# Tile 3's selection made in the front stage, and tile 3 fourth in the attention's order

## The chip, the core and the metric

The kernel runs on one core of a Trainium2 chip. Time is device time in microseconds (us). The kernel before takes 2221.42 us, the median of three runs (2221.03 to 2222.13). One more execution was taken with the hardware profiler; all rows come from it. The engines are TensorE (PE in the rows, PEld for its weight loads), VectorE (DVE), ScalarE (ACT), GpSimd (POOL), and SyncE (SP), which here only issues transfers.

## What is computed

One layer over 2048 tokens of width 1024: a projection, three mixers whose outputs are joined (a causal convolution, a sparse attention and a pooling mixer), an output projection, and a mixture of experts. The change touches the attention. Each query scores all allowed keys with eight small indexer heads, keeps the 256 best, and attends to those alone:

```python
def block(args):
    qa, qib, wib, bi = args
    qchunk = (bi * Q_BLOCK + jnp.arange(Q_BLOCK)) // CHUNK
    allowed = key_chunk[None, :] <= qchunk[:, None]
    rel = jax.nn.relu(jnp.einsum('bqhd,bsd->bqhs', qib, ki).astype(jnp.float32))
    score = jnp.einsum('bqhs,bqh->bqs', rel, wib.astype(jnp.float32)) * idx_scale
    score = jnp.where(allowed[None], score, -jnp.inf)
    _, idx = lax.top_k(score, topk)
    kv_sel = jax.vmap(lambda a, i: a[i])(ckv, idx)
    logits = jnp.einsum('bqhc,bqkc->bqhk', qa, kv_sel).astype(jnp.float32) * att_scale
    valid = (idx // CHUNK) <= qchunk[None, :, None]
    logits = jnp.where(valid[:, :, None, :], logits, -jnp.inf)
    p = jax.nn.softmax(logits, axis=-1).astype(kv_sel.dtype)
    return jnp.einsum('bqhk,bqkc->bqhc', p, kv_sel)
```

The kernel does not gather keys: it finds for each query the score of the 256th best key, and adds a mask (0, or a large negative number) to the logits of all keys.

## The kernel before

The program runs through a front stage (to about 460 us), the attention (460 to 1132), the output projection, and the experts (to 2215). The front goes three times over the tokens: convolution and pooling inputs, then latents, keys and values, and last, in `sweep3`, the indexer's queries. `sweep3` takes four chunks c of 512 tokens; for each it multiplies the reloaded activations h with weights (three matmuls for one product, lines 92 to 94: high x high, low x high, high x low parts), 96 matmuls a chunk, 384 in all, into small PSUM banks called sm. ScalarE takes the high part of each result (qsh), VectorE the low part (qsl), and both are written to DRAM (qi_d of the chunk, line 597). The front's convolution (line 630, an add of one tap over 512 tokens, on VectorE) and its transposes and normalisation run beside.

The attention has 16 query tiles of 128 queries; tile t sees (t + 1) x 128 keys. Per tile there are four parts, written as generators that yield after each step:

- `scores` loads the queries (qi, line 857), and for each of eight heads and each block of 512 keys does two matmuls (lines 862, 863), a relu on ScalarE (rel, line 865) and a weighted sum on VectorE (into S, line 866).
- `threshold` finds the 256th best: mean and deviation (line 892), five tries, each a count of the entries over a guess (tries 0 and 2 a Sign on ScalarE, the others line 922 on VectorE) and a chain of small operations on GpSimd that makes the next guess; then an exact pick (ScalarE line 957, VectorE line 958 and MAX8, line 961) and the mask (line 966).
- `logits`, for two heads at a time (a group g): loads of qa (line 1015) and kc (line 1022), matmuls (line 1028), mask and row maximum on VectorE (line 1029), Exp on ScalarE (line 1034).
- `context`: transposes of the probabilities (line 1067), copies to SBUF (pT, line 1069), products with the values vc (loaded in line 1063, multiplied in line 1054), and at the end of a tile the scaling and the write.

`attention` weaves them by a list of positions: at position p it runs the context of tile `ORDER[p]`, the logits one group ahead, the scores of `ORDER[p + 3]`, and the thresholds of `ORDER[p + 1]` and `ORDER[p + 2]`. From the second position on it also weaves in `modrows`, two steps a group: 32 loads of 512 KB of the modulation weights mod_w (line 180) and their matmuls (line 201). Tiles 0 and 1 need no selection, as they see at most 256 keys. Tile 2's is made ahead: the generator `ahead` runs its `scores` and `threshold` in `sweep3`, five steps behind each product of the chunks c > 1, in small buffers of one copy each (their names begin with e: eS, erel, ecj, ebias) and in the banks sm. All other tiles have theirs in the attention.

Tiles, pools and generators fix which instructions exist and on which buffers; a scheduler then puts each engine's instructions in one fixed order, and each engine runs its list in that order, with waits for what others produce. SyncE's transfers are such a list too: one that waits holds those behind it.

## Time and profile before

| | |
|---|---|
| median of three runs | 2221.42 us |
| profiled execution: time / span | 2217.02 / 2215.0 us |
| mean granted TensorE clock | 0.964 of full |
| busy: TensorE / VectorE / ScalarE / GpSimd | 2001.5 / 1569.5 / 1220.0 / 889.0 us |
| bytes moved, mean rate | 569.65 MB, 257 GB/s |

The profile's rows give for an instruction its line, the engine, the tiles it writes and reads (out<-in), its shape and time; in brackets the idle time of the engine just before it and what ended that. A window's row gives the busy time of each engine in that stretch, the granted TensorE clock as a share of full speed, the mean busy share of the 16 DMA engines and the rate. Tile rows run from the copy that ends one tile's context (line 1079) to the next tile's: the row of tile t then holds its context and, woven in, the next tile's logits. All positions are in us from the span's start.

### The profile page before, as it was taken

To read this page: it belongs to the slowest core of one execution; us is meant where nothing else is said; L and a number is where in the kernel's file an instruction comes from. 1 tells how busy PE (TensorE), PEld (TensorE's weight loads), DVE (VectorE), ACT (ScalarE), POOL (GpSimd) and SP (SyncE) were. 2 spreads that over 40 slices of the span, in tenths; PEclk is the share of its full clock that TensorE was granted. 3 is DMA by queue.
4 is the path that set the end of the run, shared out by engine and by line. 5 is a ranking of instruction groups with operands and counts; after the bars stand their busy time and mean duration, and the time that the engine had idled before them with its cause. 6 is when DMAs were issued, how large, how long until landed. Compare 5 with 4: busy or idle time off the path is not lost. (4 is left out here: it accounts for less than half of the span.)

```text
span 2215.0 us, 37651 instructions
## 1 busy us (share of the span) xinstructions
PE 2001.5 (90%) x12857; PEld 1509.4 (68%) x12858; DVE 1569.5 (71%) x3004; ACT 1220.0 (55%) x2039; POOL 889.0 (40%) x1599
## 2 busy tenths in 40 slices
PE   5899999988899999988889997799999999999984
PEld 4677887865667777766768775567777666666762
DVE  5696888768888888996436555666767666766673
ACT  4733333256777788877642222556666565665552
POOL 4442112446544433474000113435555455555443
PEclk9999999989999999999999998799999999999987
DMA  8636979859986666768867435799999899999894
GB/s 288 242 132 205 285 217 291 304 173 295 290 252 213 206 209 194 231 212 271 230 211 268 153 125 198 268 320 361 353 298 337 265 345 321 335 326 314 302 301 145
DMA packets 314388, 569.65 MB, mean 257 GB/s; under 512 B 36467, under 2 KB 149576, under 8 KB 313160
## 3 DMA queue, kind: packets, MB, share of 16 engines
q1 hardware_dynamic: 289560, 489.79, 66.0%
q0 software_dynamic: 22304, 68.41, 10.8%
q10 hardware_dynamic: 2320, 8.91, 1.0%
q8 instruction: 105, 1.72, 0.3%
q14 instruction: 99, 0.81, 0.1%
HBM read 462.44 MB, written 103.53 MB: 256 GB/s over the span
## 5 line engine op out<-in xcount | busy, mean ns | idle before, releaser
L1732 DVE TENSOR_TENSOR wl<-wr,wh 128x1024 fp32r<-128x1024 f32 x314 | 386.5, 1267 | 157.6 <-ACT wh L1731 151.6
L1731 ACT ACTIVATE wh<-wr 128x1024 fp32r<-128x1024 f32 x372 | 373.4, 1053 | 207.4 <-PE acc L94 162.4
L93 PE MATMUL acc<-wl,xh 128*128 128x512 f32 (+3 forms) x544 | 219.9, 405 | 4.2 <-DVE wl L1732 4.1
L1029 DVE CUSTOM_DVE_ANT_0 L<-pl,bias 128x512 f32<-128x512 f32 (+3 forms) x312 | 180.2, 607 | 60.5 <-PE pt L1067 34.0
L92 PE MATMUL acc<-wh,xh 128*128 128x512 f32 (+3 forms) x544 | 217.3, 409 | 5.4 <-ACT wh L1731 5.1
L94 PE MATMUL acc<-wh,xl 128*128 128x512 f32 (+3 forms) x544 | 216.6, 401 | 0.0
L1028 PE MATMUL pl<-kc,qa 128*128 128x512 f32 (+3 forms) x640 | 180.4, 386 | 20.2 <-DMA kc<-kh_d 9.4
L1069 ACT ACTIVATE pT<-pt 128x512 f32<-128x512 f32 (+1 forms) x288 | 158.0, 575 | 64.8 <-PE pt L1067 64.0
L1732 POOL TENSOR_TENSOR wl<-wr,wh 128x1024 fp32r<-128x1024 f32 x58 | 145.3, 2562 | 106.1 <-ACT wh L1731 104.2
L866 DVE SCALAR_TENSOR_TENSOR S<-rel,wi,S 128x512 f32<-128x512 f32 (+3 forms) x259 | 171.3, 681 | 22.5 <-ACT rel L865 21.8
L1067 PE MATMUL pt<-identr,L 128*128 128x128 f32 x1088 | 170.1, 282 | 17.2 <-ACT pT L1069 12.9
L865 ACT ACTIVATE rel<-pi 128x512 f32<-128x512 f32 (+3 forms) x296 | 153.9, 549 | 46.5 <-PE pi L863 28.8
L630 DVE SCALAR_TENSOR_TENSOR ac<-u,kc,ac 128x512 f32<-128x512 f32 x240 | 176.9, 778 | 0.1
L1067 PEld LDWEIGHTS pt<-identr,L 128*128 128x128 f32 x1088 | 126.3, 143 | 55.8 <-ACT pT L1069 22.2
L1034 ACT ACTIVATE L<-L,ast 128x128 f32<-128x128 f32 (+15 forms) x128 | 154.1, 1204 | 13.3 <-DVE ast L1033 13.0
L1054 PE MATMUL po<-pT,vc 128*64 128x128 f32 x2176 | 145.9, 281 | 12.4 <-ACT pT L1069 12.2
L1054 PEld LDWEIGHTS po<-pT,vc 128*64 128x64 f32 x2176 | 120.5, 139 | 42.0 <-ACT pT L1069 27.4
L862 PE MATMUL pi<-kk,qi 128*128 128x512 f32 (+3 forms) x296 | 127.7, 433 | 19.3 <-ACT rel L865 16.7
L1028 PEld LDWEIGHTS pl<-kc,qa 128*128 128x128 f32 x640 | 108.7, 193 | 50.2 <-DVE ast L1029 16.8
L92 PEld LDWEIGHTS acc<-wh,xh 128*128 128x128 f32 (+3 forms) x544 | 98.8, 183 | 41.9 <-ACT wh L1731 10.9
L93 PEld LDWEIGHTS acc<-wl,xh 128*128 128x128 f32 (+3 forms) x544 | 100.0, 184 | 38.6 <-issue 6.9
L1782 POOL DMA_INDIRECT x_d<-yo,ent x31 | 90.0, 2905 | 82.4 <-DVE yo L1825 57.8
(562 smaller groups left out, 4641.9 us busy)
## 6 DMA issues: line engine op xcount, KB each, us to landing
wr<-in_exp_w_dram SPq DMA_DIRECT2D x256, 512.0 KB
wr<-in_exp_w_dram SPq DMA_DIRECT2D x64, 1024.0 KB
h<-h_d SPq DMA_DIRECT2D x64, 512.0 KB
vc<-v_d SPq DMA_DIRECT2D x112, 256.0 KB
h_d<-h POOLq DMA_DIRECT2D x32, 512.0 KB
qa<-qa_d SPq DMA_DIRECT2D x128, 128.0 KB
modr<-in_mod_w_dram SPq DMA_DIRECT2D x32, 512.0 KB
xt<-in_x_dram SPq DMA_DIRECT2D x16, 512.0 KB
```

Source lines behind the costliest of these rows:

```text
L92: mm(out, lh, rh, start=start, stop=False)
L93: mm(out, lh, rl, start=False, stop=False)
L94: mm(out, ll, rh, start=False, stop=stop)
L630: nc.vector.scalar_tensor_tensor(acc[j], src, kc[:, j, i:i + 1], acc[j], op0=OP.mult, op1=OP.add)
L866: nc.vector.scalar_tensor_tensor(S[:, s:e], r[:, :e - s], self.wi[:, t, h:h + 1], S[:, s:e] if h else self.tie[:, s:e], op0=OP.mult, op1=O ...
L1028: nc.tensor.matmul(ps[:, :e - s], q[:, h % 2, m], k[:, s:e], start=m == 0, stop=m == 1)
L1029: nc.vector.tensor_tensor_reduce(L[:, s:e], ps[:, :e - s], bias[:, s:e], 1.0, -3e38, OP.add, OP.max, mx[:, i:i + 1])
L1054: nc.tensor.matmul(po[r], v[:, (k2 + i) % 4, r], pT[:, i, j], start=len(left) > 2 * t, stop=len(left) <= 2)
L1067: nc.tensor.transpose(pt[:, i, j], P[j][:, (k2 + i) * 128:(k2 + i + 1) * 128], self.ident)
L1069: nc.scalar.activation(pT[:, :m], pt[:, :m], AF.Copy)
L1731: nc.scalar.activation(H[:, s], W[:, s], AF.Copy)
L1732: (nc.gpsimd if pool else nc.vector).tensor_tensor(L[:, s], W[:, s], H[:, s].bitcast(F32), OP.subtract)
```

## The change

`ahead` makes two selections one behind the other, tile 2's and then tile 3's, advanced three steps behind each product of the chunks c = 1, 2 and 3 in place of five for c = 2 and 3. In `ORDER` tile 3 goes from the last place to the fourth. The writes of qi_d of chunk 1 go from GpSimd's queue to SyncE's. The small buffers are 512 wide in place of 384; ebias gets two copies, one for each tile; the bf16 output of the counts (cj) shares erel with the relus and the pick. `scores` in `attention` now skips tiles 0 to 3. At the position of tile 2 no scores are woven in any more; tile 8's, which stood there, stand at tile 3's.

```diff
@@ -594,9 +594,9 @@
                     for m in range(2):
                         a, b = slice(m * 64, m * 64 + 64), slice(64 - m * 64, 128 - m * 64)
                         for to, q in (a, hi), (b, lo):
-                            (nc.sync if c > 1 else nc.gpsimd).dma_start(self.qi_d[c][to, 2 * (j + i) + m, :], q[a].bitcast(F32))
-                    if c > 1:
-                        self.advance(early, 5)
+                            (nc.sync if c else nc.gpsimd).dma_start(self.qi_d[c][to, 2 * (j + i) + m, :], q[a].bitcast(F32))
+                    if c:
+                        self.advance(early, 3)
                     self.spend(side, 5)
         for _ in early:
             pass
@@ -722,7 +722,7 @@
             if "y" in self.dbg:
                 nc.sync.dma_start(self.dbg["y"][c, 2 + j], y)
 
-    ORDER = (0, 1, 2, 6, 7, 8, 9, 10, 11, 12, 13, 14, 15, 5, 4, 3)
+    ORDER = (0, 1, 2, 3, 6, 7, 8, 9, 10, 11, 12, 13, 14, 15, 5, 4)
     TRIES = 5
     SIGN = (0, 2)
 
@@ -731,20 +731,23 @@
     def work(self, pool, width, dtype, tag, bufs):
 
         if self.small:
-            tag = "e" + ("rel" if tag == "R" else tag)
-            return self.aq.tile([128, min(width, self.small)], dtype, name=tag, tag=tag,
-                                bufs=1)
+            tag = "e" + ("rel" if tag in ("R", "cj") else tag)
+            return self.aq.tile([128, min(width, 512)], dtype, name=tag, tag=tag, bufs=2 if tag == "ebias" else 1)
         return getattr(self, pool).tile([128, width], dtype, name=tag, tag=tag, bufs=bufs)
 
+    AHEAD = (2, 3)
+
     def ahead(self):
 
-        self.small, self.masks = 384, {}
-        S = self.work("ats", T, F32, "S", 1)
-        for part in self.scores(2, S), self.threshold(2, S):
-            for _ in part:
-                self.small = None
-                yield
-                self.small = 384
+        self.masks = {}
+        for t in self.AHEAD:
+            self.small = True
+            S = self.work("ats", T, F32, "S", 1)
+            for part in self.scores(t, S), self.threshold(t, S):
+                for _ in part:
+                    self.small = None
+                    yield
+                    self.small = True
         self.small = None
 
     def bank(self, tag, bufs, shape=(128, 512)):
@@ -784,7 +787,7 @@
 
             def scores(i):
 
-                if i < NT and order[i] >= 3:
+                if i < NT and order[i] > self.AHEAD[-1]:
                     t = order[i]
                     S = self.ats.tile([128, T], F32, name="S", tag="S", bufs=3)
                     thr[i] = self.threshold(t, S)
```

After the change the lines from 731 on are numbered three higher.

The scheduler's order on TensorE, at tile 2's scores in the front stage. Before (kk are the keys, qi the queries, h the activations of the products), the end of tile 2's eight heads, which stand behind 240 of the 384 products:

```order
1438 L862 MATMUL sm<-kk_1773,qi 128x384
1439 L863 MATMUL sm<-kk_1774,qi 128x384
1440 L862 MATMUL sm<-kk_1773,qi 128x384
1441 L863 MATMUL sm<-kk_1774,qi 128x384
1442 L650 MATMUL cm<-identr,ac_3179 128x128
1443 L650 MATMUL cm<-identr,ac_3180 128x128
1444 L862 MATMUL sm<-kk_1773,qi 128x384
1445 L863 MATMUL sm<-kk_1774,qi 128x384
1446 L92 MATMUL sm<-h 128x512
1447 L93 MATMUL sm<-h 128x512
```

After, the first six of tile 2's heads, which stand behind 144 products:

```order
1334 L866 MATMUL sm<-kk_1774,qi 128x384
1335 L865 MATMUL sm<-kk_1773,qi 128x384
1336 L866 MATMUL sm<-kk_1774,qi 128x384
1337 L865 MATMUL sm<-kk_1773,qi 128x384
1338 L866 MATMUL sm<-kk_1774,qi 128x384
1339 L92 MATMUL sm<-h 128x512
1340 L93 MATMUL sm<-h 128x512
1341 L94 MATMUL sm<-h 128x512
```

Tile 2's scores have moved up by 96 products, its last two heads by 48.

TensorE, the last 96 products of the front (sm<-h), after; before, nothing but products and transposes (cm) stood ahead of them here:

```order
1505 L650 MATMUL cm<-identr,ac_3179 128x128
1506 L650 MATMUL cm<-identr,ac_3180 128x128
1507 L650 MATMUL cm<-identr,ac_3179 128x128
1508 L650 MATMUL cm<-identr,ac_3180 128x128
1509 L865 MATMUL sm<-kk_1773,qi 128x512
1510 L866 MATMUL sm<-kk_1774,qi 128x512
1511 L662 MATMUL cm<-identr,lnn 128x128 x3
1512 L865 MATMUL sm<-kk_1773,qi 128x512
1513 L866 MATMUL sm<-kk_1774,qi 128x512
1514 L662 MATMUL cm<-identr,lnn 128x128 x5
1515 L92 MATMUL sm<-h 128x512
1516 L93 MATMUL sm<-h 128x512
```

Tile 3's last heads (512 keys wide) now stand ahead of them.

VectorE's order at the end of the front. Before, the end of tile 2's selection:

```order
587 L656 TENSOR_SCALAR lnn<-cm,lns 128x256
588 L653 BN_AGGR lns<-lns 128x2
589 L99 TENSOR_SCALAR lns<-lns 128x1
590 L958 SCALAR_TENSOR_TENSOR erel<-eS,esc,erel 128x384
591 L656 TENSOR_SCALAR lnn<-cm,lns 128x256
592 L961 MAX esc<-erel 128x8
593 L962 SCALAR_TENSOR_TENSOR esc<-io_3320,esc 128x8
594 L963 TENSOR_TENSOR esc<-esc 128x1
595 L88 TENSOR_TENSOR qsl<-sm,qsh 128x512
596 L966 SCALAR_TENSOR_TENSOR ebias,esc<-eS,esc,nbig 128x384
597 L88 TENSOR_TENSOR qsl<-sm,qsh 128x512
```

After, the same place of tile 2's selection:

```order
586 L969 SCALAR_TENSOR_TENSOR ebias,esc<-eS,esc,nbig 128x384
587 L653 BN_AGGR lns<-lns 128x2
588 L656 TENSOR_SCALAR lnn<-cm,lns 128x256
589 L971 TENSOR_SCALAR esc<-esc 128x1
590 L869 SCALAR_TENSOR_TENSOR eS<-erel,wi,tie 128x512
591 L99 TENSOR_SCALAR lns<-lns 128x1
592 L972 TENSOR_TENSOR esc<-esc 128x1
593 L973 TENSOR_SCALAR bad<-esc 128x1
594 L656 TENSOR_SCALAR lnn<-cm,lns 128x256
595 L869 SCALAR_TENSOR_TENSOR eS<-erel,wi,eS 128x512 x7
596 L872 MEMSET eS 64x64
```

Tile 3's first sum (eS from tie) stands behind tile 2's MAX and mask, the other seven directly behind it; before, only qsl and small operations of tile 2 followed, and then the attention.

## Rows read from the trace of the kernel before

**Rows 1.** Windows by stage and tile: us; busy us (instructions); clock, DMA share, GB/s.
```profile
375.00:460.00 85.00, 83.79 (x386) 69.18 (x384) 61.69 (x124) 17.65 (x33) 42.75 (x134) 1.00 0.80 274
509.70:546.00 36.30, 29.27 (x210) 18.85 (x210) 30.94 (x77) 24.39 (x58) 25.71 (x92) 0.95 0.96 291
546.00:595.30 49.30, 43.29 (x354) 30.70 (x353) 39.16 (x107) 34.18 (x70) 21.45 (x81) 0.97 1.00 305
595.30:636.50 41.20, 37.39 (x325) 27.57 (x326) 34.80 (x80) 30.47 (x56) 22.55 (x78) 1.00 0.86 267
958.50:1021.70 63.20, 56.30 (x475) 43.21 (x476) 52.48 (x145) 48.26 (x82) 46.47 (x187) 1.00 0.70 224
1075.70:1097.50 21.80, 19.07 (x182) 15.47 (x183) 9.59 (x42) 14.85 (x31) 0.00 (x0) 1.00 0.91 249
1097.50:1118.20 20.70, 17.10 (x152) 13.06 (x151) 8.31 (x37) 13.70 (x32) 0.00 (x0) 1.00 0.89 255
1118.20:1131.80 13.60, 11.29 (x108) 8.32 (x108) 4.04 (x17) 7.97 (x17) 0.00 (x0) 1.00 0.23 67
```

**Rows 2.** The same view, only instructions that read h, late front stage.
```profile
397.90:425.00 27.10, 22.64 (x98) 17.52 (x96) 0.00 (x0) 0.00 (x0) 0.00 (x0) 1.00 0.85 290
425.00:459.00 34.00, 33.47 (x144) 26.79 (x144) 0.00 (x0) 0.00 (x0) 0.00 (x0) 1.00 0.63 193
```

**Rows 3.** TensorE timeline: start, us, line, operation; tile 2's first and last score matmul.
```profile
420.44 0.34 PE L862 MATMUL sm<-kk,qi 128*128 128x384 f32 x1
...
424.09 0.34 PE L863 MATMUL sm<-kk,qi 128*128 128x384 f32 x1
```

**Rows 4.** VectorE timeline, 400 to 460: start, us, operation [idle before, releaser].
```profile
400.26 0.68 DVE L88 TENSOR_TENSOR qsl<-sm,qsh 128x512 fp32r<-128x512 f32 x1
400.86 1.41 DVE L630 SCALAR_TENSOR_TENSOR ac<-u,kc,ac 128x512 f32<-128x512 f32 x2
...
422.32 0.62 DVE L866 SCALAR_TENSOR_TENSOR eS<-erel,wi,tie 128x384 f32<-128x384 f32 x1 [0.36 <-ACT erel L865]
...
432.72 0.23 DVE L892 BATCH_NORM_STATS2 est<-eS 128x6 f32<-128x80 f32 x1
...
451.26 0.61 DVE L922 TENSOR_SCALAR_CACHE_REDUCE ecj<-eS,esc 128x384 bf16<-128x384 f32 x1 [2.12 <-POOL esc L940]
...
457.52 0.55 DVE L961 MAX8 esc<-erel 128x8 f32<-128x384 f32 x1
...
459.10 0.61 DVE L966 SCALAR_TENSOR_TENSOR ebias<-eS,esc,nbig 128x384 bf16<-128x384 f32 x1
```

**Rows 5.** Transfers issued in the attention's last 34 us: queue, count, KB each.
```profile
kc<-kh_d SPq DMA_DIRECT2D x8, 256.0 KB
vc<-v_d SPq DMA_DIRECT2D x5, 256.0 KB
qa<-qa_d SPq DMA_DIRECT2D x8, 128.0 KB
```

**Rows 6.** Instructions on the tile modr: count, ns min/median/max, first to last start.
```profile
L180 SPq DMA_DIRECT2D modr<-in_mod_w_dram x32: 333/356/1242, 483.0 to 623.0; - x32
```

**Rows 7.** SyncE's queue, 396 to 425: start, us to issue, line, transfer.
```profile
399.96 0.80 SPq L857 DMA_DIRECT2D qi<-qi_d  x1
...
421.34 0.61 SPq L597 DMA_DIRECT2D qi_d<-qsh  x1
```

**Rows 8.** Waits, 458 to 475: engine, tile, line, releaser, us, times, longest.
```profile
ACT rel L865 <- DMA qi_d<-qsh: 5.3, 1, 5.3
PE pi L862 <- ACT rel L865: 4.9, 1, 4.9
```

**Rows 9.** Windows of 10 us where the attention begins, columns as in the first.
```profile
460.00:470.00 10.00, 4.64 (x13) 3.34 (x14) 3.80 (x13) 2.95 (x6) 3.15 (x13) 0.64 0.76 225
470.00:480.00 10.00, 9.89 (x50) 7.22 (x49) 8.66 (x34) 8.96 (x26) 0.00 (x0) 0.85 0.49 143
```

## The prediction

> **What bounds the kernel now.** I read the windows by stage and tile first, then the timelines of TensorE and VectorE around tile 2's selection, then the waits where the attention begins, then the transfers of a short tile. In the last part of the front stage TensorE is busy 83.79 of 85 us at full clock: the front is TensorE's [rows 1], and its products come at one in 0.23 us (144 in 33.47 us [rows 2]). Whatever makes TensorE pause there lengthens the program. Tile 2's selection is free: its 16 score matmuls pass in 4.0 us [rows 3], and the rest runs on VectorE, ScalarE and GpSimd from 422.3 to 459.7 [rows 4], ending about when the last product does (at 458.5; the last 144 lie between 425 and 459 [rows 2]). In the first tiles of the attention the DMA share is 0.96 (tile 2), 1.00 (tile 6) and 0.86 (tile 7), with TensorE busy 29.27 of 36.3, 43.29 of 49.3 and 37.39 of 41.2 us [rows 1]: both are nearly full. In the last three tiles DMA has room only in the very last (0.23), and TensorE is busy 0.87, 0.83 and 0.83 of the time: no stage of this kernel is idle enough to take in a tile for nothing.
>
> **The end: what is removed.** Tiles 5, 4, 3 take 21.8 + 20.7 + 13.6 = 56.1 us [rows 1]. A tile's row holds its context and the next tile's logits; the last holds a context alone. With tile 3 gone, tile 5's row stays at 21.8 and tile 4's becomes a context without logits: 13.6 x 5/4 (five key blocks for four) = 17.0, and I add 1.5 for the waits at a drained end: 18.5. So 56.1 - 40.3 = 15.8, taken as -16 (-14 to -18). Tile 3's 16 score matmuls leave tile 14's row, where TensorE is busy 56.30 of 63.2 us and so sets the time: by [rows 3] 16 pass in 4.0 us with nine others between, 3.5 without: -3.5. Its picking (three counts, two passes, one mask, 0.55 to 0.61 us each on VectorE [rows 4]) lay in a stretch where VectorE is busy 52.48 of 63.2 us [rows 1]; most of it was covered: -1.5 (0 to -3). Sum of the end -21 (-17 to -25).
>
> **The start of the attention: what is added.** Tile 3 as fourth tile brings eight kc transfers of 256 KB, four vc of 256 KB and eight qa of 128 KB [rows 5]: 2.1 + 1.05 + 1.05 = 4.2 MB. At tile 6's 305 GB/s that is 13.8 us. Besides, the 32 loads of 512 KB of the modulation weights [rows 6], eight to a tile, now fall beside tiles 1, 2, 3, 6 in place of 1, 2, 6, 7. Tiles 2 and 6 moved 36.3 x 291 and 49.3 x 305 = 10.6 + 15.0 MB, tile 7 11.0 [rows 1]. Now tiles 2, 3, 6 need 10.6 + 15.0 + 4.2 + about 2.5 (the kc, qa and vc of the next tile that their rows prefetch) = 32.3 MB, 106 us at 305 GB/s; tile 7 without its 4.2 MB of weights still needs TensorE's 37.4 us, about 39. Together 145 against 126.8: +18. TensorE says nearly the same: tile 3's matmuls, 16 us of the end at 0.83 busy = 13.3 us, at the 0.87 of these tiles (109.95 of 126.8 us) need +15.3. I take +16. Below: had the new work packed as in tile 7 (0.91), (109.95 + 13.3) / 0.91 = 135.4, +9; above, 32.3 MB at tile 2's 291 GB/s, 111, +24.
>
> **The front: what is added.** Three things come upon TensorE. First, 16 more score matmuls, of 512 columns: 3.6 us (a fifth over [rows 3]'s width, without the transposes between). Second, tile 2's scores are asked for earlier: the rows of TensorE's order show six of its heads directly behind product 144 of 384, where before they stood behind product 240. By [rows 2] the last 144 of the 384 stand after 425.0 and 98 between 397.9 and 425.0, so product 144 is at about 398. The queries they need are loaded by a transfer on SyncE's queue, which went out at 399.96 [rows 7]; now it stands behind two writes of the second 512 queries, put on the same queue by the change, which wait for a qsl that VectorE makes at 400.26 + 0.68 [rows 4]. Writes take 0.6 us to issue [rows 7]: the load goes at about 402.5, and 512 KB in a stretch of 290 GB/s beside the reloads [rows 1, 2] arrive by about 407. TensorE pauses from 397.9 to 407: 8.5 us (4 to 12). Third, tile 3's eight heads go through one small erel buffer, which tile 2's pick also uses, and the last 96 products stand behind them. Tile 2's first sum then falls at about 408.7; each sum has two convolution steps between (0.62 + 1.41 us [rows 4], overlapped 1.9), six heads by 420, all eight and bn_stats by 423.4. From bn_stats to the end of MAX8 the trace has 432.72 to 458.07, 25.35 us of a chain in which each try waits for the one before, so MAX8 ends at 448.7. Only then can tile 3's first relu and sum follow, the third relu, which frees the banks for the products, at about 455.5. TensorE meets that point at 407 + 2.5 (six heads) + 33.1 (144 products) + 4 = 447.5: a pause of 8 us (0 to 10). The last 96 products take 22 us, 455.5 to 477.5, where before they ended at 458.5: +19.
>
> VectorE is later still: tile 3's scores end and bn_stats comes at 463.7, its last count 18.6 us on (432.72 to 451.26 in tile 2 [rows 4]), 482.5; the first sum of tile 6, which stands behind it, at 483.3 against 466.4. Here 5.3 us return: the first rel waited for the last writes from qsh, whose place its buffer takes over [rows 8]; the larger small buffers move it elsewhere, and there it waits for TensorE alone. So the attention starts +17.5 later (+4 to +22).
>
> **A rule weighed.** The trace shows what a pause does to the clock: TensorE sat 4.9 us at 461 [rows 8], and the granted clock is 0.64 in 460 to 470 and 0.85 in the next 10 us, against 1.00 in the whole of 375 to 460 [rows 1, 9]. The Trainium skill, "TensorE: Matmul & The Clock Gate", section "HAM oscillation — how this bites in real kernels", says that a TensorE that keeps waiting for transfers falls back to the half-rate clock and starts each burst cold; the trace agrees in direction (0.64). By the rows the lost clock is (0.36 + 0.15) x 10 = 5 us of full speed at most per pause, of which that beginning already pays one; two new pauses would add up to 10, which I count below as a rival and not in the sum, since after the first pause VectorE and not TensorE sets the pace. The Trainium skill, "DMA: Bandwidth & Descriptors", section "Issuing engines are not separate DMA queues", says that transfers issued from GpSimd and SyncE share the same DMA engines, so that another issuer saves issue time alone; by that rule the writes' move to SyncE's queue buys no bandwidth. No run here shows the two issuers compared, and the sum above would be the same without the rule.
>
> **Sum.** Front +17.5, start +16, end -21: +12.5 on the profiled execution's 2217.02 us, 2229.5. That execution lies 4.4 us under the median of the three runs, 2221.42; with them I predict 2234. Differences under 0.2% (4.4 us) this kernel's measurement can't tell from none.
>
> **The rivals.**
> - Faster: the products don't wait for tile 2's pick. If the banks are free in another order than I read, or tile 2's tries run quicker with VectorE less held, the second pause is nothing, and the first is the 4 us of its lower bound: front 3.6 + 4 - 5.3 = +2. With the start at its lower bound, +9: 2 + 9 - 21 = -10, 2211. It decides from a second pause under 2 us. For it: tile 2's sums waited for ScalarE and not VectorE in part; against it: the single erel buffer, which the diff states. 0.10.
> - The same: pauses of 4 each, 3.6 + 8 - 5.3 = +6, and a start of +15: 6 + 15 - 21 = 0, 2221. For it: TensorE's DMA waits in tiles 2 to 7 are far less than the share of 1.00 suggests, its busy share being 0.81 to 0.91. 0.17.
> - Slower still: the clock. Two pauses of about 8 us drop it twice, the products that follow run at part speed (+10), and the transfers keep to 291 GB/s (+24 for +16): 12.5 + 10 + 8 = +30, 2252. For it: the 0.64 above. Against: the first pause's loss lies beside VectorE. 0.13.
> - The change doesn't do what it says: tile 3's selection not ready when its logits want it, fourth in order. Its mask is wanted some 50 us after the start; its pick ends about 495 by the steps above. Little in it: 0.02, with 2240.
> - The forecast, 2234 (its own range 2226 to 2243): 0.58.
>
> Faster by over 0.2% 0.11, within 0.2% 0.17, slower 0.72. The range 2216 to 2248 leaves out the better part of the first rival and of the clock's.
>
> **What would show it.** In the profile after: two idle spells of TensorE between 395 and 460, the first ended by the queries' transfer, the second by ScalarE's erel, 5 to 10 us each; the last product at 474 to 480; the first sum of S at about 483; tiles 2, 3, 6, 7 in 140 to 147 us at a DMA share of 0.95 and more; the last two tiles of the attention in about 40 us. I am wrong if the last product ends before 466, if tile 3 costs the start under 10 us, or if the last two tiles take over 46.

## The result, and the profile after

The changed kernel takes 2241.05 us (median of five runs, 2231.44 to 2250.68) against 2221.03 for the kernel before on the same chip: ratio 1.0091, interval 1.0069 to 1.0114. It is slower, by 15 to 25 us. Run again beside other kernels it gave 1.0094 (1.0069 to 1.0119). The kernel before itself has medians of 2213.1, 2213.5 and 2219.8 us on the three chips of the experiments, so ratios are always taken on one chip, and positions in two profiles compare to a few us only.

The profiled execution took 2239.95 us with a span of 2238.2, 23.2 more than before. First the windows of the stretches that answer to [rows 1]: the late front stage, tiles 2, 3, 6, 7, tile 14, and the last two tiles, 5 and 4. Columns as there: us, busy time by engine, granted clock, DMA share, GB/s.

```profile
375.00:460.00 85.00, 72.65 (x313) 59.60 (x312) 60.22 (x125) 18.49 (x34) 35.96 (x124) 0.90 0.77 269
528.90:555.80 26.90, 20.23 (x155) 10.63 (x154) 16.13 (x48) 12.88 (x32) 18.14 (x84) 0.81 0.96 299
555.80:592.70 36.90, 32.83 (x238) 21.96 (x238) 29.65 (x75) 25.75 (x59) 10.54 (x34) 0.91 0.94 292
592.70:641.00 48.30, 43.21 (x350) 30.28 (x350) 39.76 (x101) 33.32 (x68) 24.57 (x79) 1.00 0.95 308
641.00:679.00 38.00, 33.85 (x274) 27.10 (x275) 31.86 (x79) 30.82 (x60) 18.73 (x70) 1.00 0.72 216
1000.40:1063.50 63.10, 54.95 (x459) 43.37 (x458) 49.16 (x140) 44.61 (x74) 38.52 (x155) 0.95 0.71 236
1110.60:1131.70 21.10, 18.93 (x182) 15.38 (x183) 9.50 (x42) 14.90 (x31) 0.00 (x0) 1.00 0.88 258
1131.70:1148.90 17.20, 14.68 (x144) 11.56 (x143) 5.52 (x28) 10.77 (x25) 0.00 (x0) 1.00 0.34 98
```

In the late front stage TensorE is busy 72.65 of 85 us where it had been 83.79, at clock 0.90. Tiles 2, 3, 6, 7 take 26.9 + 36.9 + 48.3 + 38.0 = 150.1 us against 126.8 for tiles 2, 6, 7, at a DMA share of 0.94 to 0.96 in the first three. Tile 14 takes what it took, and the last tiles 38.3 in place of 56.1.

Now the front. TensorE's timeline (start, us, line, operation, in brackets the idle time before and what ended it), rows with idle time and the first of the last 96 products:

```profile
405.77 0.69 PE L865 MATMUL sm<-kk,qi 128*128 128x384 f32 x1 [8.30 <-DMA qi<-qi_d]
...
449.99 0.41 PE L650 MATMUL cm<-identr,ac 128*128 128x128 f32 x2 [1.90 <-DVE lnn L656]
...
453.04 0.88 PE L662 MATMUL cm<-identr,lnn 128*128 128x128 f32 x3 [1.27 <-DVE esc L971]
454.30 0.80 PE L865 MATMUL sm<-kk,qi 128*128 128x512 f32 x1 [0.38 <-ACT erel L868]
...
456.29 0.80 PE L92 MATMUL sm<-h 128*128 128x512 f32 x1
```

The first pause is 8.30 us, for the queries' transfer. The second is a group of short ones from 447.7 to 456.29, in which only four score matmuls and some transposes pass, at a falling clock (the first product behind it takes 0.80 us, 0.39 elsewhere). The profile puts these on VectorE's lnn and esc, and on ScalarE's erel. ScalarE's first three relus of tile 3 show what lies under them:

```profile
450.34 0.60 ACT L868 ACTIVATE erel<-sm 128x512 f32<-128x512 f32 x1 [1.61 <-DVE esc L964]
453.65 0.60 ACT L868 ACTIVATE erel<-sm 128x512 f32<-128x512 f32 x1 [2.71 <-DVE eS L869]
455.64 0.60 ACT L868 ACTIVATE erel<-sm 128x512 f32<-128x512 f32 x1 [1.39 <-DVE eS L869]
```

The first waits for tile 2's MAX8 (line 964), which still reads erel; each of the next waits for the sum that empties erel. They end at 450.94, 454.25 and 456.24, and TensorE's next matmuls into the banks sm start at 451.06, 454.30 and 456.29. The products end at 479.2 + 0.4 us, as the row of the products' last form says (count, ns min/median/max, first and last start); before, this was 458.5.

```profile
L94 PE MATMUL sm<-h,wl x71: 389/389/400, 375.1 to 479.2; 128*128 128x512 f32 x71
```

VectorE's timeline, the rows that answer to [rows 4]: tile 2's first sum, bn_stats, last count and MAX8, then tile 3's first and last sum and last count, then tile 6's first two sums.

```profile
407.34 0.62 DVE L869 SCALAR_TENSOR_TENSOR eS<-erel,wi,tie 128x384 f32<-128x384 f32 x1 [0.32 <-ACT erel L868]
...
424.65 0.23 DVE L895 BATCH_NORM_STATS2 est<-eS 128x6 f32<-128x80 f32 x1
...
444.07 0.61 DVE L925 TENSOR_SCALAR_CACHE_REDUCE erel<-eS,esc 128x384 bf16<-128x384 f32 x1 [3.61 <-POOL esc L943]
...
449.76 0.55 DVE L964 MAX8 esc<-erel 128x8 f32<-128x384 f32 x1
...
452.87 0.74 DVE L869 SCALAR_TENSOR_TENSOR eS<-erel,wi,tie 128x512 f32<-128x512 f32 x1
...
463.77 0.75 DVE L869 SCALAR_TENSOR_TENSOR eS<-erel,wi,eS 128x512 f32<-128x512 f32 x1 [0.67 <-ACT erel L868]
...
484.74 0.75 DVE L925 TENSOR_SCALAR_CACHE_REDUCE erel<-eS,esc 128x512 bf16<-128x512 f32 x1 [2.99 <-POOL esc L943]
...
485.95 1.28 DVE L869 SCALAR_TENSOR_TENSOR S<-rel,wi,tie 128x512 f32<-128x512 f32 x2
```

Tile 2's chain from bn_stats to the end of MAX8 takes 25.7 us (424.65 to 450.31; 25.35 before). Tile 3's first sum follows 2.6 us behind, its last count ends at 485.5, and tile 6's first sum starts at 485.95 in place of 466.38. SyncE's queue shows the load of tile 2's queries behind the writes from qsl:

```profile
399.33 1.08 SPq L597 DMA_DIRECT2D qi_d<-qsl  x2
400.72 0.58 SPq L860 DMA_DIRECT2D qi<-qi_d  x1
```

Then the attention starts badly: TensorE waits for the first kc, and goes on at a granted clock of about half (windows of 10 us, and the wait).

```profile
480.00:490.00 10.00, 3.47 (x14) 2.34 (x13) 5.94 (x17) 2.79 (x6) 7.09 (x30) 0.81 0.66 167
490.00:500.00 10.00, 7.95 (x26) 5.75 (x24) 7.16 (x29) 6.62 (x16) 2.30 (x13) 0.51 0.50 136
```

```profile
PE pl L1031 <- DMA kc<-kh_d: 5.8, 1, 5.8
```

Tile 0 ends at 507.7 (484.3 before, +23.4), tile 1 at 528.9 (509.7, +19.2), tile 7 at 679.0 (636.5, +42.5), tile 13 at 1000.4 (958.5, +41.9), the last tile at 1148.9 (1131.8, +17.1). The remaining 6.1 us of the 23.2 lie behind the attention, where nothing was changed. They are no effect that I can claim: the same changed kernel, profiled twice, took 1089.3 and 1081.4 us there.

```profile
1148.90:2238.20 1089.30, 997.61 (x6175) 720.20 (x6175) 706.04 (x981) 535.60 (x741) 456.30 (x265) 0.95 0.82 278
```

```profile
1152.30:2233.70 1081.40, 989.78 (x6175) 715.70 (x6175) 699.23 (x981) 535.41 (x741) 451.10 (x265) 0.96 0.82 280
```

### The profile page after: what moved, and what is told of

It is laid out like the page before. It is cut to its first block, busy times and chain, and to the rows that moved or that the text cites. A ratio compares the mean times of both kernels' runs of the same rounds, so it can differ in the third digit from the quotient of the medians.

```text
span 2238.2 us, 37628 instructions
## 1 busy us (share of the span) xinstructions
PE 2016.1 (90%) x12857; PEld 1516.8 (68%) x12858; DVE 1570.3 (70%) x3004; ACT 1219.3 (54%) x2039; POOL 881.8 (39%) x1583
## 5 line engine op out<-in xcount | busy, mean ns | idle before, releaser
L1032 DVE CUSTOM_DVE_ANT_0 L<-pl,bias 128x512 f32<-128x512 f32 (+3 forms) x304 | 175.3, 604 | 60.1 <-PE pt L1070 32.8
L1031 PE MATMUL pl<-kc,qa 128*128 128x512 f32 (+3 forms) x640 | 186.1, 394 | 22.0 <-DMA kc<-kh_d 14.8
L1070 PE MATMUL pt<-identr,L 128*128 128x128 f32 x1088 | 172.3, 284 | 23.3 <-ACT pT L1072 15.1
L1072 ACT ACTIVATE pT<-pt 128x512 f32<-128x512 f32 (+1 forms) x288 | 157.9, 576 | 57.2 <-PE pt L1070 56.1
L869 DVE SCALAR_TENSOR_TENSOR S<-rel,wi,S 128x512 f32<-128x512 f32 (+3 forms) x252 | 166.7, 681 | 25.8 <-ACT rel L868 25.4
L868 ACT ACTIVATE rel<-pi 128x512 f32<-128x512 f32 (+3 forms) x288 | 150.2, 548 | 46.1 <-PE pi L866 24.1
L1037 ACT ACTIVATE L<-L,ast 128x128 f32<-128x128 f32 (+15 forms) x128 | 154.1, 1204 | 23.4 <-DVE ast L1036 21.6
```

The costliest lines, as they stand in the source:

```text
L869: nc.vector.scalar_tensor_tensor(S[:, s:e], r[:, :e - s], self.wi[:, t, h:h + 1], S[:, s:e] if h else self.tie[:, s:e], op0=OP.mult, op1=O ...
L1031: nc.tensor.matmul(ps[:, :e - s], q[:, h % 2, m], k[:, s:e], start=m == 0, stop=m == 1)
L1032: nc.vector.tensor_tensor_reduce(L[:, s:e], ps[:, :e - s], bias[:, s:e], 1.0, -3e38, OP.add, OP.max, mx[:, i:i + 1])
L1070: nc.tensor.transpose(pt[:, i, j], P[j][:, (k2 + i) * 128:(k2 + i + 1) * 128], self.ident)
L1072: nc.scalar.activation(pT[:, :m], pt[:, :m], AF.Copy)
```

## The experiments

All ratios are against the kernel before on the same chip, with their 95% intervals. The last tile's end is that of the profile; before, 1131.8.

| kernel | ratio | interval | last tile's end |
|---|---|---|---|
| changed | 1.0091 | 1.0069 to 1.0114 | 1148.9 |
| changed, again | 1.0094 | 1.0069 to 1.0119 | 1152.3 |
| order alone | 0.9953 | 0.9934 to 0.9971 | 1127.1 |
| front alone | 1.0086 | 1.0060 to 1.0112 | 1148.5 |
| own buffers | 1.0069 | 1.0046 to 1.0092 | 1144.6 |
| writes on GpSimd | 1.0153 | 1.0130 to 1.0177 | 1164.1 |
| begun later | 1.0022 | 1.0005 to 1.0039 | 1143.4 |
| changed, loads late | 1.0004 | 0.9991 to 1.0017 | 1135.9 |
| before, loads late | 0.9996 | 0.9978 to 1.0013 | 1130.8 |
| order alone, loads late | 0.9973 | 0.9956 to 0.9990 | 1126.7 |
| own buffers, loads late | 0.9999 | 0.9980 to 1.0018 | 1126.8 |
| all three | 1.0014 | 0.9996 to 1.0032 | 1131.0 |

**Order alone and front alone.** The change was taken apart in two. In the first, only the list of positions was edited in the kernel before; tile 3 then gets its scores beside tile 0's context:

```diff
-    ORDER = (0, 1, 2, 6, 7, 8, 9, 10, 11, 12, 13, 14, 15, 5, 4, 3)
+    ORDER = (0, 1, 2, 3, 6, 7, 8, 9, 10, 11, 12, 13, 14, 15, 5, 4)
```

> The kernel before with the new ORDER alone: tile 3 fourth, its selection in the attention like every other tile's, the front stage untouched. First theory (the pauses in the front are the loss, and the move of tile 3 by itself is nearly even: tiles 2, 3, 6, 7 took 23 us more in the kernel after, the last tiles 25 less): the attention begins as before (first sum of S at 466), the start costs +20 to +23 and the 4 us of tile 3's score matmuls, the end gives 25; total -1 to +6 us against before, ratio 0.9995 to 1.003. Rival (the transfers at the start cost more than the end gives, whatever the front does): +8 us or more, ratio 1.004 and up. Second rival (the end's gain is real and the start absorbs tile 3): -8 us or better.

It is faster than before, 0.9953 (0.9934 to 0.9971): the second rival came out, by size, and the first theory's -1 was too cautious. Its windows for tiles 1 to 9 (with 3), tiles 10 to 14, and the last three:

```profile
485.00:750.60 265.60, 239.52 (x1823) 172.21 (x1823) 223.06 (x579) 196.09 (x389) 150.31 (x532) 0.94 0.84 259
750.60:1041.10 290.50, 261.28 (x2149) 208.50 (x2150) 244.68 (x596) 230.31 (x390) 121.69 (x460) 0.99 0.68 219
1041.10:1127.10 86.00, 77.97 (x766) 64.04 (x766) 36.77 (x144) 60.43 (x105) 0.00 (x0) 1.00 0.70 217
```

Tiles 1 to 9 take 265.6 us against 249.9 before, +15.7; the last three take 86.0 where 15, 5, 4, 3 took 110.1, -24.1. The move is worth having when the front stage is left alone.

The second is the changed kernel with the old list (the same line, reversed).

> The changed kernel with the old ORDER: tiles 2 and 3 are selected in the front stage, but tile 3 stays last in the attention. First theory: the front costs what it costs in the changed kernel (last product at 479, first sum of S at 486, +19), tiles 1 to 7 are as before, and the end wins only tile 3's score matmuls and picking, 4 to 9 us; total +10 to +16 us against before, ratio 1.0045 to 1.007. Rival (the lateness at the front is made good by the attention, whose VectorE then has less to do): under +6 us, ratio below 1.003.

Ratio 1.0086, more than the 1.0045 to 1.007 expected: last product at 480.0, tile 6's first sum at 487.4, the last tile's end at 1148.5, +16.7. Here tile 15 takes 48.0 us in place of 54.0 and tile 14 62.0 in place of 63.2, which is all that the selection's removal gives. The first theory holds in its account, and the attention makes up nothing of the lateness beyond that. So the order gains and the selection in the front stage loses.

The two do not simply add. By the profiles, -4.7 and +16.7 make +12.0 at the last tile's end, where the changed kernel has +17.1. Tile 15's relief accounts for it: it is in both parts (54.0 us before, 47.3 and 48.0 here) and the changed kernel has it once (47.1). By the ratios the gap is larger, +0.0039 against +0.0091, and the rest of it is not located.

**Own buffers for tile 2.** Scores' sum, counts and pick of tile 2 in three buffers of the front's weight pool, so that erel and eS are free for tile 3 (the lines that keep self.now and self.wp3 are left out here):

```diff
+            if self.now == 2 and tag in ("R", "cj", "S"):
+                return self.wp3.tile([128, 384], dtype, name="f" + tag, tag="f" + tag, bufs=1)
             tag = "e" + ("rel" if tag in ("R", "cj") else tag)
```

> The changed kernel, in which tile 2's score sum, counts and pick have small buffers of their own in the front stage's weight pool, so that tile 3's relus and sums need not wait for tile 2's MAX and mask. First theory (second pause made by the shared buffers): TensorE's second pause shrinks from about 6 us to under 2, the last product ends at 473 to 475 in place of 479.5, the total is 4 to 8 us under the changed kernel, ratio 1.0055 to 1.0075. Rival (the chain of tile 2's tries on VectorE, with the convolution's normalisation queued behind it, makes the pause): last product at 478 or later, ratio 1.008 to 1.010.

The row of the products in this kernel's profile:

```profile
L94 PE MATMUL sm<-h,wl x71: 387/389/395, 375.1 to 471.0; 128*128 128x512 f32 x71
```

The last product starts at 471.0 in place of 479.2, and TensorE's only pause between 390 and 472 is the first, 8.15 us: the second is gone, and with it 8.2 us. So tile 2's pick, by the buffers that it holds, made the second pause. The rival (the chain queued on VectorE by itself) is out, as the chain ends no earlier here: MAX8 starts at 450.63, at 449.76 in the changed kernel.

```profile
450.63 0.56 DVE L967 MAX8 esc<-fR 128x8 f32<-128x384 f32 x1
```

The edit is not quite clean, since the order of the lists moves with it: the transposes of lnn for which TensorE waited ahead of the last 96 products stand behind most of them here. Tile 0 ends 10.6 us earlier than in the changed kernel. Over the whole, 4.3 us of this were left at the attention's end, and 1.0069 was measured, as expected, though its interval overlaps the changed kernel's. Tiles 12 and 13 took 132.1 us in place of 123.6, with TensorE waiting 6.4 us for ScalarE's pT in tile 13. The order of the engines' lists differs there too, and the cause is open: over all the kernels here these two tiles take 118.8 to 133.6 us.

**Writes left on GpSimd's queue.**

```diff
-                            (nc.sync if c else nc.gpsimd).dma_start(...)
+                            (nc.sync if c > 1 else nc.gpsimd).dma_start(...)
```

> The changed kernel with the writes of the second 512 queries left on GpSimd's queue, as before the change, so that the load of tile 2's queries on SyncE's queue has no write ahead of it that waits for VectorE. First theory (the first pause, 8.3 us, is made by those writes): the load goes at 396 to 399 in place of 403, TensorE's first pause is 3 to 5 us, total 3 to 6 us under the changed kernel, ratio 1.006 to 1.008. Rival (the queries of tile 2 are simply not yet in DRAM: their own writes and the 512 KB take that long): the pause stays at 7 us or more, ratio 1.008 to 1.010.

By the ratio both theories failed: 1.0153, slower than the changed kernel. On the pause the rival was right, 7.1 us. The load of the queries left at 398.74, two us earlier than in the changed kernel, and the pause was one us shorter. SyncE's queue shows what held it (who waited for what: us, times, longest): the queries of the first 512 tokens were not yet written.

```profile
SPq L860 <- DMA qi_d<-qsl: 12.3, 2, 12.0
```

The load's place behind the second chunk's writes cost 1 to 2 of the 8.3 us; the rest is that tile 2's scores are asked for when its queries are just being written, and the transfer itself. What made the front slower is that tile 2's chain of guesses runs later. GpSimd has eight writes to issue (four in 2.11 us, two in 1.03, and two more) before the chain's first operation, and then waits for ScalarE's first count (line 922). Here, and then in the changed kernel:

```profile
420.58 2.11 POOL L597 DMA_DIRECT2D qi_d<-qsh  x4 [15.71 <-ACT qsh L87]
422.68 1.03 POOL L597 DMA_DIRECT2D qi_d<-qsl  x2
...
427.13 0.57 POOL L898 TENSOR_TENSOR esc<-esc,phalf 128x1 f32<-128x1 f32 x1
...
432.99 0.19 POOL L923 TENSOR_SCALAR esc<-esc 128x1 f32<-128x1 f32 x1 [3.66 <-ACT erel L922]
```

```profile
425.19 0.56 POOL L898 TENSOR_TENSOR esc<-esc,phalf 128x1 f32<-128x1 f32 x1 [0.87 <-DVE esc L896]
...
428.22 0.19 POOL L923 TENSOR_SCALAR esc<-esc 128x1 f32<-128x1 f32 x1 [0.82 <-ACT erel L922]
```

The first count on VectorE stands at 435.66 here and at 429.88 in the changed kernel:

```profile
435.66 0.61 DVE L925 TENSOR_SCALAR_CACHE_REDUCE erel<-eS,esc 128x384 bf16<-128x384 f32 x1 [1.54 <-POOL esc L934]
```

```profile
429.88 0.61 DVE L925 TENSOR_SCALAR_CACHE_REDUCE erel<-eS,esc 128x384 bf16<-128x384 f32 x1 [4.78 <-POOL esc L934]
```

Of these 5.8 us the chain's first operation has 1.9, the writes' share. The longer wait for ScalarE has 2.8: its list has a qsh (at 431.72) ahead of that count here, which waits for products, and behind it in the changed kernel. The last 1.0 comes with a write of y_d that stands on GpSimd's queue inside the chain. MAX8 follows 6.7 us later, the last 96 products resume at 461.2 in place of 456.3, and the last starts at 484.6. So with shared buffers the second pause follows the chain's end.

This makes about 6 of the 15 us by which the attention ends later; the other 10 come in tiles 12 and 13 (133.6 us in place of 123.6), as with own buffers, and are open. In this kernel the writes were better on SyncE's queue, not for the load's sake but for the chain. It is not so in general: the last two kernels of the table differ in this edit alone, and there the last product starts no later with the writes on GpSimd's queue (469.0) than with them on SyncE's (472.7), and the intervals do not tell the ratios apart (1.0014 and 0.9999).

**Begun later.** The selections ahead advance only behind chunk 2 and 3, as tile 2's did before:

```diff
-                    if c:
-                        self.advance(early, 3)
+                    if c > 1:
+                        self.advance(early, 5)
```

(with the writes of chunk 1 on GpSimd's queue)

> The changed kernel with the selections ahead begun only behind chunk 1 as in the kernel before, five steps behind each product of the chunks 2 and 3, and the writes of chunk 1 on GpSimd's queue as before; the rest of the steps follow behind the last product. First theory (the first pause comes from asking for tile 2's scores 96 products earlier): no wait for qi on TensorE, the last product at 462 to 470; but tile 3's sums and first tries then stand between the products and tile 6's first sum, at 474 to 482; total 6 to 14 us under the changed kernel, ratio 1.003 to 1.006. Rival (the selection's end and not its beginning decides): as the changed kernel, 1.008 to 1.011.

TensorE waits for no queries; but the second pause is now longer and stands bare, 8.15 us for ScalarE's erel:

```profile
460.05 0.80 PE L865 MATMUL sm<-kk,qi 128*128 128x512 f32 x1 [8.15 <-ACT erel L868]
...
462.09 0.80 PE L865 MATMUL sm<-kk,qi 128*128 128x512 f32 x1 [0.82 <-ACT erel L868]
...
463.51 0.80 PE L92 MATMUL sm<-h 128*128 128x512 f32 x1 [0.20 <-ACT erel L868]
```

The last product starts at 475.8, 6 us later than the latest that I expected, tile 6's first sum at 483.40. MAX8 starts 9.0 us later than in the changed kernel (458.80), and the pause ends behind it again. Ratio 1.0022 (1.0005 to 1.0039), some 13 to 16 us under the changed kernel and more than the first theory expected; the rival is out. The attention's end, 1143.4, shows only 6 to 9 of these, so part of it isn't located.

**Loads of the modulation weights two tiles later**, in the changed kernel, the kernel before, the order alone, and with own buffers:

```diff
-                           (b1, 2), (b2, 1 + g % 2), *([(rows, 2)] if p else []))
+                           (b1, 2), (b2, 1 + g % 2), *([(rows, 2)] if p > 2 else []))
```

> The changed kernel with the 32 loads of modulation weights begun two tiles later, beside tiles 3, 6, 7, 8 in place of 1, 2, 3, 6: tiles 7 and 8 showed DMA shares of 0.72 and 0.64. First theory (the stretch of tiles 2, 3, 6 is set by its 33.7 MB at about 300 GB/s): tiles 1 to 8, 217 us in the changed kernel, take 205 to 210; total 7 to 12 us less, ratio 1.004 to 1.006. Rival (TensorE's own work and waits for ScalarE pace these tiles, the transfers fill in beside): 217 within 3, ratio 1.008 to 1.010.

In the changed kernel this wins nearly all of the loss back, 1.0004 (0.9991 to 1.0017). Tiles 1 to 9 in the changed kernel, and with late loads:

```profile
507.70:770.70 263.00, 231.83 (x1813) 166.33 (x1813) 212.21 (x549) 192.65 (x383) 131.30 (x471) 0.96 0.83 260
```

```profile
512.40:761.00 248.60, 230.49 (x1818) 167.19 (x1818) 212.16 (x553) 192.47 (x384) 135.13 (x471) 0.98 0.87 276
```

248.6 us in place of 263.0, for the same matmuls and the same bytes, with a DMA share of 0.87 in place of 0.83. The loads' place cost 14 us in these tiles, a little over the 7 to 12 expected. How much of that came with tile 3, the kernel before has to show.

> The kernel before with the loads of modulation weights begun two tiles later (beside tiles 6, 7, 8, 9 in place of 1, 2, 6, 7). First theory (transfers set the pace of the first tiles in the kernel before too, where tiles 2 and 6 showed shares of 0.96 and 1.00): 4 to 10 us less, ratio 0.9955 to 0.998. Rival (only with tile 3 there do they exceed what the stretch can take): within 2 us, ratio 0.999 to 1.001.

In the kernel before it wins nothing, 0.9996, and yet the first tiles are faster here too. Tiles 1 to 9 and 10 to the end, before and with late loads:

```profile
484.30:734.20 249.90, 219.67 (x1698) 159.31 (x1697) 205.65 (x526) 182.50 (x357) 132.51 (x471) 0.97 0.84 259
734.20:1131.80 397.60, 360.52 (x3040) 286.42 (x3040) 300.74 (x794) 307.46 (x532) 142.55 (x538) 0.99 0.70 218
```

```profile
484.60:723.90 239.30, 217.87 (x1695) 157.17 (x1695) 205.52 (x525) 181.15 (x357) 135.27 (x471) 0.98 0.87 267
723.90:1130.80 406.90, 365.63 (x3044) 291.75 (x3044) 299.74 (x795) 307.43 (x531) 143.31 (x538) 0.97 0.68 215
```

10.6 us less in the first stretch, 9.3 more in the second, with a clock of 0.97 in place of 0.99 and 0.02 lower DMA share. The transfers did set the pace of the first tiles, as the first theory had it, but what follows gave it back. So 10.6 of the 14.4 us lay in these tiles before tile 3 came there, and only about 4 are new, hardly more than the 2.8 us by which this stretch differs between the two profiles of the changed kernel. Why the gain was kept in the changed kernel and given back in this one I don't know.

> The new ORDER alone, with the loads of modulation weights begun two tiles later; no second selection in the front stage. First theory (the move of tile 3 and the spreading of the loads add up): 14 to 24 us less than before, ratio 0.989 to 0.9935. Rival (the loads only move the crowding to tiles 7 and 8, which the order alone had already sped up): as the order alone, ratio 0.9945 to 0.997.

The order alone with late loads gave 0.9973: worse than the order alone (0.9953), if by no more than the intervals allow. Tiles 1 to 9 took 261.9 us, only 3.7 less. The two gains don't add; the rival is nearer.

Set side by side, these stretches show how the parts hang together. With the loads in their old place tiles 1 to 9 take 265.6 us with tile 3's selection in them (order alone) and 263.0 without it (changed). With late loads they take 261.9 and 248.6. So taking the selection out of these tiles is worth 2.6 us while the transfers fill them and 13.3 once they don't. By the ratios the selection in the front costs 0.0138 in the first case and 0.0031 in the second.

> The changed kernel with own buffers for tile 2's selection and the loads of modulation weights two tiles later, the writes of chunk 1 on SyncE's queue as in the change. First theory (the two gains add: the pause of 8 us and the crowding): last product at 471, ratio 0.996 to 0.999. Rival (the tries on VectorE ahead of tile 6's first sum are the bound left, whichever pause goes): ratio 0.999 to 1.002, as with the late loads alone.

Own buffers with late loads gave 0.9999, with the last product at 472.7 and the first sum of tile 6 at 478.24. The profile's attention ends at 1126.8, as if the gains added, but the median does not show it: by the median the rival is right.

> The changed kernel with all three: own buffers for tile 2's selection, the second 512 queries' writes on GpSimd's queue, the loads of modulation weights two tiles later. First theory (these three make the loss, and making tile 3's selection in the front is then worth the 4 us of matmuls and the picking taken out of the first tiles): the last product at 464 to 468, ratio 0.990 to 0.997. Rival (the selection in the front still delays the attention by its chain on VectorE, whose last count stands ahead of tile 6's first sum): first sum of S at 473 or later and a ratio of 0.996 to 1.001, worse than the order with late loads alone.

All three together (own buffers, the writes on GpSimd's queue, late loads) gave 1.0014, with the last product at 469.0 and the first sum at 477.45. The rival is right in its account, and the ratio lies just above its range: with the second pause gone and the first at 7.1, tile 6's first sum still comes 11 us later than before, as tile 3's counts stand ahead of it. After that the granted clock is 0.50 from 475 to 495. Tile 2's MAX8 starts as late here (456.67) as with the writes on GpSimd's queue alone (456.48), and yet there is no second pause: the buffers make it.

**The changed kernel again.**

> The changed kernel once more, on the same chip as what it is compared with here. First theory: as measured before, ratio 1.007 to 1.011. Rival (the chip made part of the difference between it and the runs with late loads): under 1.005.

The ratio is 1.0094 again, so the rival is out. Positions repeat less well: TensorE starts tile 2's scores at 409.55 in this profile and at 405.77 in the other, and all that follows is about 3 us later too (last product 482.3, last tile's end 1152.3).

## Why the prediction was right

It was right in sign and range: 2234 predicted, with 2216 to 2248, 2241 measured. Compared by the profiles, term by term (us; the first four rows are a length and positions, the others differences from the kernel before):

| term | predicted | measured | where |
|---|---|---|---|
| first pause | 8.5 | 8.3 | TensorE, 405.77 |
| products go on | 455.5 | 456.29 | TensorE |
| last product ends | 477.5 | 479.6 | row of h |
| tile 6's first sum | 483.3 | 485.95 | VectorE |
| attention's start | +17.5 | +19.2 | tile 1's end |
| tiles 2, 3, 6, 7 | +16 | +23.3 | windows |
| tiles 8 to 13 | 0 | -0.6 | tile 13's end |
| tiles 14 to the last | -21 | -24.8 | windows |
| behind the attention | 0 | +6.1 | not the change's |
| sum | +12.5 | +23.2 | |

**The front** was right step by step, within 3 us everywhere. The second pause is made by the shared small buffers (own buffers removed it and 8.2 us), and with them it follows the end of tile 2's chain of tries (with MAX8 6.7 us later it came five later; begun later it stood bare at 8.15 us). The third relu of tile 3, which the prediction had as the one that frees the banks, at about 455.5, started at 455.64. The prediction's sum for the point where TensorE stops is off by 0.9 (407 + 2.5 + 33.1 + 4 is 446.6 and not 447.5); the last score matmul ahead of the pause started at 447.70. Of the two idle spells of 5 to 10 us that were to show it, the second came in four pieces, with 4.05 us of idle time in all. The first pause has the right length with one part left out: the load could not have gone before about 398.7, as the queries' own writes hold it until then (writes on GpSimd's queue). The writes put ahead of it cost 2.0 us of its start, where the prediction had 2.5, and 1.2 us of the pause; from the load's start to TensorE's it took 5.05 us, where the prediction had 4.5. VectorE's sum, 483.3 against 466.4, is +16.9; how it became +17.5 the prediction doesn't say. Tile 6's first sum came 0.5 us behind the end of tile 3's last count, so that the 5.3 us of the first rel's old wait could not show in it.

**The start** is the term that was mis-sized, +16 for +23.3, and the tiles' 150.1 us lie outside the 140 to 147 that were to show it. Between the two estimates, +18 and +15.3, I took a value nearer the lower. Tiles 2, 3, 6 moved 33.7 MB (26.9 x 299 + 36.9 x 292 + 48.3 x 308) where I had 32.3, in 112.1 us where I had 106: 301 GB/s, under the 305 of tile 6 on which I built. The 1.4 MB more make 4.6 of these 6 us, the rate the rest. Tile 2, which has lost its scores, ran at clock 0.81 and TensorE's busy share fell to 0.75; tile 3 at 0.91. The upper end that I gave, +24, is nearly what came. That transfers pace these tiles is shown by the late loads, 14.4 us less in tiles 1 to 9 with the same work; but most of that (10.6) was to be had in the kernel before too, so they do not show that tile 3's transfers are all of the +23.3.

**The end** gave a little more, -24.8 for -21: tile 15 took 47.1 us in place of 54.0, so that tile 3's picking was not mostly covered, as I had it (-1.5), but cost about 6 there (the front alone and the order alone show the same, 48.0 and 47.3). The score matmuls' 3.5 us in tile 14 don't show: TensorE's busy time there falls from 56.30 to 54.95, at a clock of 0.95 in place of 1.00. So the start came out 7 us dearer and the end 4 us cheaper than worked out; that these two errors partly cancel in the sum is luck. At the attention's end the change costs 17.1 us, of the 20.0 between the medians.

**The rivals.** The faster one needed a second pause under 2 us; it was a group that cost 8.2 us, and even without it the kernel is slower (own buffers, 1.0069). The clock's rival was partly in it: the clock is 0.51 from 490 to 500 and 0.81 in tile 2, and tile 0's end is 4 us later than the start of its sums explains. Tile 1 gives those 4 back (21.2 us for 25.4), so that I count none of it at the end. The Trainium skill's rule on a TensorE that waits and then runs cold ("TensorE: Matmul & The Clock Gate", "HAM oscillation — how this bites in real kernels") agrees with these rows in direction: the granted clock is 0.50 in the 5 us in which TensorE starts again behind the wait for the queries' transfer, and 0.61 in the 5 us behind the second pause, whose waits were for ScalarE and VectorE and not for transfers; it was 1.00 from 440 to 450.

```profile
405.00:410.00 5.00, 4.23 (x13) 4.23 (x14) 4.68 (x9) 1.07 (x3) 0.20 (x1) 0.50 0.52 165
455.00:460.00 5.00, 5.00 (x18) 3.99 (x17) 2.54 (x4) 3.02 (x5) 1.21 (x3) 0.61 0.59 202
```

The other rule that I weighed, that the issuing queue buys no bandwidth ("DMA: Bandwidth & Descriptors", "Issuing engines are not separate DMA queues" in the Trainium skill), agrees too as far as the load goes: 5.05 us from its start to TensorE's with the writes on SyncE's queue, 5.5 with them on GpSimd's. What the engines' lists hold decided here: with eight writes on GpSimd's queue the chain's arithmetic began 1.9 us later, and its first count on VectorE came 5.8 later, as ScalarE's list had changed too.

**A version that beats both** came from taking the change apart: the new order without the selection in the front, 0.9953 of the kernel before. Tiles 1 to 9 take 265.6 us there and 263.0 in the changed kernel: with tile 3's selection beside them they are only 2.6 us longer, and the front is about 20 us shorter (tile 6's first sum at 465.5, by its profile, for 485.95).

## What to carry to other kernels

Work that fills an idle engine is free only as long as nothing on the full engine is queued behind it: ask of each shared buffer and bank which instruction of the bound engine stands next in line, and work out when the chain before it ends. A change of two parts should be priced and run in its parts: here the order alone gains 0.5% and the preparation made for it loses more than that. Gains and losses of the parts may overlap, as tile 15's relief did, so the parts don't replace a run of the whole. Work taken out of a stretch pays by what bounds the stretch: tile 3's selection was worth 2.6 us in tiles 1 to 9 while transfers filled them, and 13.3 with the loads moved away. When a tile is moved into a stretch whose transfers are full, count the stretch's bytes again, with what else was placed there for its idle time.

## What was not expected of the hardware

Eight writes of 128 KB took GpSimd about 0.5 us each to issue and put off the chain of 0.2 us operations behind them by 1.9 us; the chain's first count came 5.8 us later, most of it because ScalarE's list was ordered anew. Late loads made tiles 1 to 9 10.6 us shorter in the kernel before and the whole no faster. Tiles 12 and 13 take 118.8 to 133.6 us in kernels that give them the same work, and the cause is open. The stretch behind the attention, unchanged in all kernels, took 1089.3 and 1081.4 us in two executions of one program, as much as some of the effects sought.
